# The last blocks of a decoder layer's final stage in two column halves, its final norm scaled on ScalarE and applied in groups of blocks

## The chip, the cores and the metric

One Trainium2 chip, all 8 cores. Each core computes 1024 of the 8192 positions by itself, in two parts of 512 positions. The metric is the device time in microseconds (us) of the slowest core.

A run of all cores is fast or slow: in a slow run the cores of one die (cores 0 to 3 or 4 to 7), or of both, show a lower granted TensorE clock than the others, and the time is longer. Even a fast run can hold a dip of the clock on two cores that costs about 26 us (before's profiled run: 6695.6 and 6695.2 us on cores 4 and 5, 6662.8 to 6679.3 on the six others), and all the effects below are no larger than that. I therefore also read one stretch of each trace, the **last stage**: from the start of the 128x512 fp32 matmul that sums the squares of the first part (it ends that part) to the end of the span. In the trace of the kernel before, this stretch is 287.4 to 287.7 us on all eight cores, while the spans of the same eight cores differ by 33 us. It is a difference of two times in one trace, core by core.

## The reference, cut to what matters

```python
# last sub-layer of the layer (D = 4096, 32 blocks of 128 channels)
ple_gate = sigmoid(rms_norm(x, norm_ple_gate) @ w_ple_gate)      # 4096 x 4096
x = x + rms_norm(ple_gate * (p @ w_ple), norm_ple_post)
```

The post norm needs the sum of squares over all 4096 channels of a position. So no channel of the output can be finished before the last block of the gate matmul is done.

## The kernel before

Channels are on the 128 partitions (32 blocks), positions on the columns. Every weight block is streamed through a ring of 12 slabs of 256 KB whose loads GpSimd issues; x and the output go through SyncE. The program gives each engine its own list of instructions, and in the traces an engine works it off in order: in x5 below the same VectorE instructions in another order take 3.28 us a block in place of 4.95. In the views TensorE is PE, VectorE is DVE, ScalarE is ACT and GpSimd is POOL; PSUM (ps) is the memory that the matmuls write. rstd is the factor that a norm multiplies with, the reciprocal root of the mean square.

```python
def e_job(hf, f, side):              # block f of part hf: 32 + 2 matmuls of 128x512
    bg, be = one_bank(512), one_bank(512)
    def evac_g():                    # gate = sigmoid(psum * rstd)
        O("dve", "tensor_tensor", ... in0=pv(bg), in1=r4.v, op=ALU.mult)
        O("act", "activation", ... func=AF.Sigmoid)
        ...                          # very last block: a tiny Ln, to load its table early
    def evac_e():
        r = R3[hf][f] = alloc(f"R3{hf}_{f}", [512], F32)
        O("dve", "tensor_tensor", ... out=r.v, in0=pv(be), in1=sg.v, op=ALU.mult)
        ...                          # squares: ScalarE Square, then acc += on VectorE
        if f == NCH - 1:
            ...
            if hf == 0:              # first part: its norm runs as "side" steps between
                B.side.extend(last(0, ...))          # the second part's matmuls
                B.side.extend(load_x2(k) for k in range(NKEEP))
    ...

# norm_steps, as used by last(): two VectorE instructions of 128x512 per block
def scaled(k): O("dve", "tensor_tensor", ... in0=m, in1=r.v, op=ALU.mult)
def added(k):  O("dve", "scalar_tensor_tensor", ... in0=m, scalar=gains[:, gp, k:k + 1],
                 in1=x.v, op0=ALU.mult, op1=ALU.add)

for f in range(NCH): e_job(0, f, 14)
for f in range(NCH): e_job(1, f, 14)
B.code(tail)                         # second part: its whole norm after the last matmul
```

The softmax here doesn't subtract the row's maximum and nothing guards it: scores larger than these inputs give would overflow.

## Time and profile before

| | before |
|---|---|
| time, fast runs | 6670.8 to 6671.2 us |
| TensorE busy | 98% of the span |
| chain of waits | 95% TensorE |
| last weight matmul, from the start of the last stage | 237.3 us |
| from there to the end (the tail) | 50.1 us |

The page's first part (busy time, share, instructions) and fourth part (the chain that ended last), kernel before:

```profile
PE 6561.1 (98%) x41283; PEld 4030.5 (60%) x41283; DVE 1975.1 (29%) x2585; ACT 828.2 (12%) x1248; POOL 1352.8 (20%) x2531
...
PE 95%; DMA 1%; DVE 1%; ACT 1%; issue 1%; POOL 0%; DVEq 0%; ACTq 0%; SPq 0%; POOLq 0%
```

The chain says that nearly all of the time is matmuls behind matmuls. What is not is at the two ends. The end, in the timeline of core 4 (start, duration, engine, operation, output and inputs, shape, count; in brackets the engine's idle time before it and what ended it):

```profile
6407.95 1.10 PE L144 MATMUL ps<-sb_arena,sb_ones_f 128*128 128x512 f32 x2 [2.23 <-DVE sb_arena L144]
...
6638.80 1.10 PE L144 MATMUL ps<-sb_arena,sb_ones_f 128*128 128x512 f32 x2 [1.83 <-DVE sb_arena L144]
6639.73 5.56 PE L144 MATMUL ps<-sb_arena,sb_wr 128*128 128x512 bf16 x25
...
6644.97 0.69 DVE L144 TENSOR_TENSOR sb_arena<-ps,sb_arena 128x512 f32<-128x512 f32 x1 [6.42 <-PE ps L144]
6645.75 0.63 ACT L144 ACTIVATE sb_arena<-sb_arena 128x512 f32<-128x512 f32 x1 [8.07 <-DVE sb_arena L144]
6646.40 1.28 ACT L144 ACT_TABLE_LOAD   x1
...
6648.56 0.59 PE L144 MATMUL ps<-sb_arena,sb_ones_b 128*128 128x512 bf16 x1 [3.27 <-ACT sb_arena L144]
...
6650.76 1.29 DVE L144 TENSOR_TENSOR sb_arena<-sb_arena 128x512 f32<-128x512 f32 x2 [3.58 <-ACT sb_arena L144]
6651.97 0.74 DVE L144 SCALAR_TENSOR_TENSOR sb_arena<-sb_arena,sb_cf 128x512 f32<-128x512 f32 x1
...
6689.90 1.40 DVE L144 SCALAR_TENSOR_TENSOR sb_arena<-sb_arena,sb_cf 128x512 f32<-128x512 f32 x2
```

The first line starts the last stage; the second is the fp32 sum of squares of the second part, which waited 1.83 us. The last weight matmuls end near 6645 us. Then comes a chain through VectorE, ScalarE (with a table load of 1.28 us) and one small matmul to 6650.8, and from there 64 VectorE instructions, two a block: 6650.76 to 6691.3 and 40.5 us long. `norm_steps` puts the product of the next block ahead of the sum of this one, so that no instruction needs the result of the one just before it. The last store lands at 6695.6.

The windows view of the same core (start:end, length, busy time and count of PE, PEld, DVE, ACT, POOL, then the granted clock, the DMA share and GB/s):

```profile
6525.00:6550.00 25.00, 25.00 (x117) 11.35 (x116) 7.37 (x12) 5.04 (x8) 9.39 (x18) 1.00 1.01 305
6600.00:6625.00 25.00, 25.00 (x118) 11.30 (x116) 7.20 (x11) 4.41 (x7) 8.76 (x18) 1.00 0.57 166
6650.00:6675.00 25.00, 0.00 (x0) 0.00 (x0) 24.24 (x39) 0.63 (x1) 0.00 (x0) 0.50 0.46 178
```

TensorE is full until the tail, VectorE is full in the tail (24.24 of 25 us) and mostly idle before it. The DMA engines are full (share 1.01) while x and the first part's output move, and at 0.57 when only weights do.

This profiled run itself is no measure of the total: core 4 took 6695.6 us, 24 us more than the timed runs, because its granted clock was 0.81 for 100 us and 0.89 for another 100 (windows view, 500 to 700 us).

### The profile page before, as it was taken

What the parts mean: (1) busy time and instruction counts of PE and PEld (TensorE: products, weight loads), DVE (VectorE), ACT (ScalarE), POOL (GpSimd) and SP (SyncE); (2) the same over time, 40 slices, a digit from 0 to 9 for tenths busy, and PEclk for the clock granted to TensorE, in tenths of its full rate; (3) what the DMA queues carried; (4) which work ended last, traced back from release to release, by engine and by line L of the source; (5) the groups of instructions that cost most, each with busy time, mean ns of one, the idle gap of its engine ahead of it and who ended that gap; (6) DMA issues with size and microseconds to landing.
All of it is one profiled execution on the core that took longest, in us unless ns stands there. A gap on an engine that the chain in (4) does not pass through costs nothing.

```text
span 6695.6 us, 104771 instructions; the slowest of 8 cores (6662.8 to 6695.6 us)
## 1 busy us (share of the span) xinstructions
PE 6561.1 (98%) x41283; PEld 4030.5 (60%) x41283; DVE 1975.1 (29%) x2585; ACT 828.2 (12%) x1248; POOL 1352.8 (20%) x2531
## 2 busy tenths in 40 slices
PE   6999999999999999999999999999999999999996
PEld 4656666666665585866644566665446666544443
DVE  3432311111111125433300133332013333334454
ACT  2550000000001233000000000000000000013311
POOL 1111111111112322311111111111111111233332
PEclk9998999999999999999999999999999999999998
DMA  7557988899887587688899988556875555589885
GB/s 180 82 77 95 116 114 114 117 122 120 116 115 170 158 225 218 176 112 109 110 146 161 156 114 111 77 77 119 163 142 77 77 76 76 138 229 262 236 243 189
DMA packets 377185, 923.25 MB, mean 138 GB/s; under 512 B 49920, under 2 KB 72576, under 8 KB 370944
## 3 DMA queue, kind: packets, MB, share of 16 engines
q0 software_dynamic: 290016, 717.91, 66.2%
q1 hardware_dynamic: 86400, 197.94, 9.5%
q8 instruction: 337, 5.52, 0.3%
q14 instruction: 144, 1.18, 0.1%
q10 hardware_dynamic: 288, 0.70, 0.0%
HBM read 1310.05 MB, written 206.61 MB: 227 GB/s over the span
## 4 chain that ended last, share of the span: by engine, by line
PE 95%; DMA 1%; DVE 1%; ACT 1%; issue 1%; POOL 0%; DVEq 0%; ACTq 0%; SPq 0%; POOLq 0%
PE ps L144 95%; DVE sb_arena L144 1%; ACT sb_arena L144 1%; DMA sb_arena<-w_in 1%; DMA sb_arena<-xs 1%; POOL sb_arena L144 0%; DVEq L143 0%; ACTq L143 0%; ACT L144 0%; DVEq L132 0%; ACT sb_warm L144 0%; SPq L143 0%; POOLq L169 0%
## 5 line engine op out<-in xcount | busy, mean ns | idle before, releaser
L144 PE MATMUL ps<-sb_arena,sb_wr 128*128 128x512 bf16 (+5 forms) x39744 | 6410.8, 323 | 7.5 <-DVE sb_arena L144 4.4
L144 PEld LDWEIGHTS ps<-sb_arena,sb_wr 128*128 128x128 bf16 x39744 | 3890.5, 98 | 2434.0 <-issue 12.8
L144 DVE TENSOR_TENSOR sb_arena<-ps,sb_arena 128x512 f32<-128x512 f32 (+10 forms) x904 | 684.1, 757 | 3995.1 <-PE ps L144 3796.4
L144 ACT ACTIVATE sb_arena<-sb_arena 128x512 f32<-128x512 f32 (+11 forms) x686 | 494.1, 723 | 4627.9 <-DVE sb_arena L144 4511.8
L144 POOL DMA_DIRECT2D sb_wr<-w_up x608 | 322.2, 530 | 1750.5 <-PE ps L144 1679.6
L144 DVE TENSOR_TENSOR sb_arena<-sb_arena 128x512 f32<-128x512 f32 (+8 forms) x545 | 449.6, 837 | 532.6 <-ACT sb_arena L144 503.9
L144 DVE SCALAR_TENSOR_TENSOR sb_arena<-sb_arena,sb_cf 128x1024 f32<-128x1024 f32 (+4 forms) x576 | 593.2, 1031 | 40.8 <-DVE sb_arena L144 0.9
L144 POOL DMA_DIRECT2D sb_wr<-w_in x384 | 205.0, 541 | 1295.7 <-PE ps L144 1295.7
L144 POOL DMA_DIRECT2D sb_wr<-w_down x256 | 135.7, 530 | 666.6 <-PE ps L144 641.7
L144 ACT ACTIVATE sb_arena<-ps 128x512 bf16<-128x512 f32 (+7 forms) x291 | 160.2, 550 | 777.4 <-PE ps L144 770.3
L144 PE MATMUL ps<-sb_arena 128*128 128x296 bf16 (+4 forms) x1216 | 182.0, 267 | 30.4 <-DVE sb_arena L144 17.4
L144 POOL DMA_DIRECT2D sb_wr<-b_out x256 | 137.5, 537 | 339.9 <-PE ps L144 316.4
L144 DVE TENSOR_SCALAR sb_arena<-sb_arena,sb_cf 128x1024 f32<-128x1024 f32 (+3 forms) x320 | 183.5, 602 | 55.5 <-PE ps L144 20.2
L144 POOL DMA_DIRECT2D sb_wr<-b_down x256 | 137.6, 537 | 283.5 <-PE ps L144 251.2
L144 POOL DMA_DIRECT2D sb_wr<-b_pg x256 | 137.6, 537 | 232.2 <-PE ps L144 215.9
L144 PEld LDWEIGHTS ps<-sb_arena 128*128 128x128 bf16 (+1 forms) x1216 | 107.9, 98 | 106.2 <-issue 74.8
L144 POOL DMA_DIRECT2D sb_wr<-b_up x160 | 86.2, 538 | 203.4 <-PE ps L144 190.9
L144 PE MATMUL ps<-sb_arena,sb_ones_b 128*128 128x296 bf16 (+3 forms) x289 | 75.1, 338 | 42.5 <-ACT sb_arena L144 21.4
L144 ACT ACTIVATE sb_arena<-ps,sb_cf 64x386 f32<-64x386 f32 (+3 forms) x112 | 69.8, 624 | 287.1 <-PE ps L144 283.0
L144 ACT ACTIVATE sb_arena<-sb_arena,sb_cf 128x512 bf16<-128x512 f32 (+1 forms) x128 | 90.7, 708 | 0.0
L144 DVE TENSOR_TENSOR sb_arena<-sb_arena,sb_cb 128x512 bf16<-128x512 bf16 (+1 forms) x192 | 64.3, 335 | 65.4 <-ACT sb_arena L144 59.7
L144 POOL DMA_DIRECT2D sb_wr<-w_bp x64 | 33.8, 528 | 194.2 <-PE ps L144 190.6
(31 smaller groups left out, 251.5 us busy)
## 6 DMA issues: line engine op xcount, KB each, us to landing
sb_wr<-w_up POOLq DMA_DIRECT2D x608, 256.0 KB, 4.3
sb_wr<-w_in POOLq DMA_DIRECT2D x384, 256.0 KB, 6.2
sb_wr<-b_out POOLq DMA_DIRECT2D x256, 256.0 KB, 3.0
sb_wr<-b_pg POOLq DMA_DIRECT2D x256, 256.0 KB, 6.5
sb_wr<-w_down POOLq DMA_DIRECT2D x192, 256.0 KB, 6.3
sb_wr<-b_down POOLq DMA_DIRECT2D x192, 256.0 KB, 3.7
sb_wr<-b_up POOLq DMA_DIRECT2D x160, 256.0 KB, 3.8
b_out<-w_out POOLq DMA_DIRECT2D x32, 1024.0 KB, 14.1
```

The lines of the kernel that those rows point to most:

```text
L144: inst = getattr(engine, fn[0])(**fn[1])
```

## The change

The intent is to shorten the tail. The last 8 blocks of the second part are computed in two column halves, first all eight blocks for 256 columns, then all eight for the other 256; their gate weights are read twice. The norm of the first half can then run beside the matmuls of the second half, and only 256 columns are left for the tail. The gain is multiplied in earlier, on ScalarE, so the last two instructions per element are a plain product and a plain sum, done for four blocks at a time (128x1024), the sum right behind its own product (`fin`); in the tail, groups 0 and 4 of eight are given to GpSimd.

```diff
+        NLAST = 8
+        HW = 256
...
+        def half_job(h, f, last, side):            # block f, columns of half h
+            bg = one_bank(HW)
+            be = one_bank(512) if h == 0 else None # w_ple for both halves, once
...
+                gate(pv(bg), bg[0][0], 1, cols, sg)          # VectorE product, ScalarE sigmoid
...
+                    O("dve", "tensor_tensor", [t.b, sg.b], [t.b], ..., op=ALU.mult)
+                if last:
+                    ...                                      # Square in bf16
+                    B.side.extend(last_B(h, last_rstd(h), (t, ap, f)))
+                else:
+                    O("act", "activation", ..., func=AF.Square)
+                    scale_gain(t, ap, f)                     # ScalarE: r *= gain
+                    O("dve", "tensor_tensor", ..., op=ALU.add)   # acc += squares
...
+        def fin(eng, R, x, r, put):                          # a group's final norm
+            O(eng, "tensor_tensor", [R.b, r.b], [R.b], ..., op=ALU.mult)
+            O(eng, "tensor_tensor", [R.b, x.b], [R.b], ..., op=ALU.add)
+            put()
...
+            if h == 0:
+                for g in range(8):
+                    out.append(step(g, "dve"))
+                    if g >= XE:
+                        out.append(load_xb(1, g))
+                return out
+            order = ((0, "pool"), (1, "dve"), (2, "dve"), (3, "dve"), (4, "pool"), (5, "dve"), ...)
...
-        for f in range(NCH):
-            e_job(1, f, 14)
-        B.code(tail)
+        for f in range(NCH - NLAST):
+            e_job(1, f, 24)
+        for f in range(NCH - NLAST, NCH):
+            if f == NCH - 1:
+                B.code(B.drain_side)
+                B.code(lambda: B.side.append(sum_most(0)))   # fp32 sum of the squares so far
+            half_job(0, f, f == NCH - 1, 24)
+        for f in range(NCH - NLAST, NCH):
+            if f == NCH - 1:
+                B.code(lambda: B.side.appendleft(sum_most(1)))
+            half_job(1, f, f == NCH - 1, 18)                 # a side step every 18 matmuls
+        B.code(B.drain_side)
```

The first part's norm is rewritten in the same way (groups of two blocks of 512, all on VectorE).

More of the change, by code (lines that the diff above doesn't have):

```diff
@@ L390, in build_nc @@
         O("dve", "memset", [], [constB], partial=True, ap=ones_b[:], constant=1.0)
+        onesB = constB
         O("dve", "memset", [], [constB], partial=True, ap=ones_f[:], constant=1.0)
@@ L856, in added @@
                     O("act", "activation", [m.b], [q.b], out=q.v, in_=m.v[:, 0:n], func=AF.Square)
-                    h = hout[k] = alloc(f"h_{k}", [n], BF16)
+                    h = hout[k] = alloc(f"h_{k}", [n], BF16, hi=gn == 4)
                     O("act", "activation", [m.b, constB], [h.b], out=h.v, in_=m.v[:, 0:n], func=AF.Copy,
@@ L1150, in build_nc @@
             down_part(1, f, 22)
-        R3 = [{}, {}]
+        NLAST = 8
+        HW = 256
         outB = []
+        RA = {}
+        RB = [{}, {}]
+        XB = [{}, {}]
         def start_E():
@@ L1160, in start_E, with sum_most, run, last_rstd @@
             G["sg"] = [alloc(f"sg{i}", [512], F32, hi=True) for i in range(3)]
+            G["sql"] = [alloc(f"sql{h}", [HW], BF16, hi=True) for h in range(2)]
         warm, warmB = sb("warm", [128, 1], F32)[:], Buf("warm")
-        def sum_most():
-            O("pe", "matmul", [G["acc"].b, constB], [psB[7]], out=ps[:, 7, 0:512], lhsT=ones_f[:], rhs=G["acc"].v,
-              start=True, stop=False)
-        def last_rstd(r):
-            O("pe", "matmul", [G["sqf"].b, constB], [psB[7]], partial=True, out=ps[:, 7, 0:512], lhsT=ones_b[:],
-              rhs=G["sqf"].v.bitcast(BF16)[:, 0:512], start=False, stop=True)
-            rstd_to(r, [(7, 0, 512, 0)])
+        def sum_most(h):
+            def run():
+                O("pe", "matmul", [G["acc"].b, constB], [psB[6 + h]], out=ps[:, 6 + h, 0:HW], lhsT=ones_f[:],
+                  rhs=G["acc"].v[:, h * HW:(h + 1) * HW], start=True, stop=False)
+            return run
+        def last_rstd(h):
+            def run(r):
+                O("pe", "matmul", [G["sql"][h].b, onesB], [psB[6 + h]], partial=True, out=ps[:, 6 + h, 0:HW],
+                  lhsT=ones_b[:], rhs=G["sql"][h].v, start=False, stop=True)
+                rstd_to(r, [(6 + h, 0, HW, 0)])
+            return run
+        def r_of(hf, f):
+            if hf == 0:
+                if f % 2 == 0:
+                    RA[f // 2] = alloc(f"RA{f}", [2, 512], F32)
+                t = RA[f // 2]
+                return [(t, t.v[:, f % 2, :], slice(0, 512))]
+            out = []
+            for h in range(2):
+                if f // 4 not in RB[h]:
+                    RB[h][f // 4] = alloc(f"RB{h}_{f}", [4, HW], F32)
+                t = RB[h][f // 4]
+                out.append((t, t.v[:, f % 4, :], slice(h * HW, (h + 1) * HW)))
+            return out
+        def gate(ap, bank, hf, cols, sg):
+            r4 = G["r4"][hf]
+            n = cols.stop - cols.start
+            O("dve", "tensor_tensor", [psB[bank], r4.b], [sg.b], out=sg.v[:, 0:n], in0=ap, in1=r4.v[:, cols], op=ALU.mult)
+            O("act", "activation", [sg.b], [sg.b], out=sg.v[:, 0:n], in_=sg.v[:, 0:n], func=AF.Sigmoid)
+        def scale_gain(t, ap, f):
+            O("act", "activation", [t.b, constB], [t.b], partial=True, out=ap, in_=ap, func=AF.Copy,
+              scale=gains[:, 5, f:f + 1])
         def e_job(hf, f, side):
@@ L1176, in evac_g @@
             def evac_g():
-                sg, r4 = G["sg"][f % 3], G["r4"][hf]
-                O("dve", "tensor_tensor", bufs(bg) + [r4.b], [sg.b], out=sg.v, in0=pv(bg), in1=r4.v, op=ALU.mult)
-                O("act", "activation", [sg.b], [sg.b], out=sg.v, in_=sg.v, func=AF.Sigmoid)
-                if (hf, f) == (1, NCH - 1):
-                    O("act", "activation", [constB], [warmB], out=warm, in_=epst[:, 0:1], func=AF.Ln)
+                gate(pv(bg), bg[0][0], hf, slice(0, 512), G["sg"][f % 3])
             def evac_e():
@@ L1187, in evac_e @@
                     G["sqf"] = alloc("sqf", [512], F32, hi=True)
-                r = R3[hf][f] = alloc(f"R3{hf}_{f}", [512], F32)
                 sg = G["sg"][f % 3]
-                O("dve", "tensor_tensor", bufs(be) + [sg.b], [r.b], out=r.v, in0=pv(be), in1=sg.v, op=ALU.mult)
-                if (hf, f) == (1, NCH - 1):
-                    O("act", "activation", [r.b], [G["sqf"].b], out=G["sqf"].v.bitcast(BF16)[:, 0:512], in_=r.v,
-                      func=AF.Square)
-                else:
-                    squares(r, 512, G["acc"], G["sqf"], f == 0)
-                if f == NCH - 1:
-                    B.drain_side()
-                    free([h2[hf][c] for c in range(NCH)])
-                    if hf == 0:
-                        free(G["sqf"])
-                    if hf == 0:
-                        B.side.extend(last(0, acc_rstd(G["acc"], ((0, 512),))))
-                        B.side.extend(load_x2(k) for k in range(NKEEP))
-            if (hf, f) == (1, NCH - 1):
-                B.code(lambda: B.side.appendleft(sum_most))
+                ps_ = r_of(hf, f)
+                for t, ap, cols in ps_:
+                    O("dve", "tensor_tensor", bufs(be) + [sg.b], [t.b], partial=True, out=ap,
+                      in0=ps[:, be[0][0], cols], in1=sg.v[:, cols], op=ALU.mult)
+                acc, sqf = G["acc"], G["sqf"]
+                d = acc if f == 0 else sqf
+                for t, ap, cols in ps_:
+                    O("act", "activation", [t.b], [d.b], partial=cols.start > 0, out=d.v[:, cols], in_=ap, func=AF.Square)
+                    scale_gain(t, ap, f)
+                if f > 0:
+                    O("dve", "tensor_tensor", [sqf.b, acc.b], [acc.b], out=acc.v, in0=acc.v, in1=sqf.v, op=ALU.add)
+                if hf == 0 and f == NCH - 1:
+                    B.drain_side()
+                    free([h2[0][c] for c in range(NCH)], sqf)
+                    B.side.extend(last_A(acc_rstd(acc, ((0, 512),))))
+                    B.side.extend(load_xb(h, g) for h, g in xb_early)
             B.one(B.chunk(bg, NCH, lambda k, h: h2[hf][k].v, lambda k: [h2[hf][k].b], evac_g),
@@ L1211, in e_job @@
                           evac_e), B.slabs("w_ple", f, 2))
-        def last(hf, acc):
-            t0 = hf * 512
-            def res(k, t):
-                if hf == 0:
-                    O("sp", "dma_start", [x2B[0][k]], [t.b], dma=f"xin{k % NR}", out=t.v, in_=x2_d[k][:, 0:512])
-            def put(k, m):
-                b = Buf(f"out{hf}_{k}")
-                outB.append(b)
-                O("sp", "dma_start", [m.b], [b], dma=f"out{k % 8}", out=out_d[k][:, t0:t0 + 512], in_=m.v)
-            return norm_steps(512, ((0, 512),), R3[hf], acc, 5, res, put, None, None, lambda: None,
-                              xs=None if hf == 0 else X2)
@@ L1228, in build_nc, with evac, evac_e @@
-        X2 = {}
-        NKEEP = 22
-        def load_x2(k):
+        def half_job(h, f, last, side):
+            bg = one_bank(HW)
+            be = one_bank(512) if h == 0 else None
+            cols = slice(h * HW, (h + 1) * HW)
+            def evac():
+                sg = G["sg"][f % 3]
+                gate(pv(bg), bg[0][0], 1, cols, sg)
+                if last:
+                    O("act", "activation", [onesB], [warmB], out=warm, in_=epst[:, 0:1], func=AF.Ln)
+                t, ap, _ = r_of(1, f)[h]
+                if h == 0:
+                    O("dve", "tensor_tensor", bufs(be) + [sg.b], [t.b], partial=True, out=ap,
+                      in0=ps[:, be[0][0], 0:HW], in1=sg.v[:, 0:HW], op=ALU.mult)
+                else:
+                    O("dve", "tensor_tensor", [t.b, sg.b], [t.b], partial=True, out=ap, in0=ap, in1=sg.v[:, 0:HW],
+                      op=ALU.mult)
+                if last:
+                    q = G["sql"][h]
+                    O("act", "activation", [t.b], [q.b], out=q.v, in_=ap, func=AF.Square)
+                    B.due = 0
+                    B.side.extend(last_B(h, last_rstd(h), (t, ap, f)))
+                else:
+                    O("act", "activation", [t.b], [G["sqf"].b], out=G["sqf"].v[:, 0:HW], in_=ap, func=AF.Square)
+                    scale_gain(t, ap, f)
+                    a = G["acc"]
+                    O("dve", "tensor_tensor", [G["sqf"].b, a.b], [a.b], partial=True, out=a.v[:, cols], in0=a.v[:, cols],
+                      in1=G["sqf"].v[:, 0:HW], op=ALU.add)
+            def evac_e():
+                t, ap, c1 = r_of(1, f)[1]
+                O("act", "activation", bufs(be), [t.b], partial=True, out=ap, in_=ps[:, be[0][0], c1], func=AF.Copy)
+            if h == 0:
+                B.one(B.chunk(be, 2, lambda k, h_: G["pT"][k].v[:, 512:1024], lambda k: [G["pT"][k].b], evac_e),
+                      B.slabs("w_ple", f, 2))
+            B.one(B.chunk(bg, NCH, lambda k, h_: h2[1][k].v[:, cols], lambda k: [h2[1][k].b], evac),
+                  B.slabs("b_pg", f, NCH, cast=G["c_pg"][f]), side=side)
@@ new lines, in fin, with rep_rstd, row @@
+        def fin(eng, R, x, r, put):
+            O(eng, "tensor_tensor", [R.b, r.b], [R.b], out=R.v, in0=R.v, in1=r.v, op=ALU.mult)
+            O(eng, "tensor_tensor", [R.b, x.b], [R.b], out=R.v, in0=R.v, in1=x.v, op=ALU.add)
+            put()
+            free(R, x)
+        def rep_rstd(r, w, n):
+            for i in range(1, n):
+                O("dve", "tensor_copy", [r.b], [r.b], partial=True, out=r.v[:, i, :], in_=r.v[:, 0, :])
+        def row(t, n):
+            v = Tl()
+            v.b, v.v = t.b, t.v[:, 0, :]
+            return v
@@ new lines, in last_A, with ld, start, step @@
+        def last_A(rstd):
+            S = {}
+            def ld(g):
+                if g < NCH // 2:
+                    S[g] = alloc(f"xA{g}", [2, 512], F32, hi=True)
+                    O("sp", "dma_start", [x2B[0][2 * g], x2B[0][2 * g + 1]], [S[g].b], dma=f"xin{g % NR}",
+                      out=S[g].v, in_=x2_d[2 * g:2 * g + 2, :, 0:512].rearrange("k p t -> p k t"))
+            def start():
+                S["r"] = alloc("rpA", [2, 512], F32, hi=True)
+                for g in range(3):
+                    ld(g)
+                rstd(row(S["r"], 512))
+                rep_rstd(S["r"], 512, 2)
+            def step(g):
+                def run():
+                    def put():
+                        b = Buf(f"outA{g}")
+                        outB.append(b)
+                        O("sp", "dma_start", [RA[g].b], [b], dma=f"out{g % 8}",
+                          out=out_d[2 * g:2 * g + 2, :, 0:512].rearrange("k p t -> p k t"), in_=RA[g].v)
+                    fin("dve", RA[g], S[g], S["r"], put)
+                    ld(g + 3)
+                    if g == NCH // 2 - 1:
+                        free(S["r"])
+                return run
+            return [start] + [step(g) for g in range(NCH // 2)]
@@ L1232, in run, with load_xb @@
+        def load_xb(h, g):
             def run():
-                t = X2[k] = alloc(f"x2r{k}", [512], F32)
-                O("sp", "dma_start", [x2B[1][k]], [t.b], dma=f"xk{k % 8}", out=t.v, in_=x2_d[k][:, 512:1024])
-            return run
+                t = XB[h][g] = alloc(f"xB{h}{g}", [4, HW], F32, hi=True)
+                c0 = 512 + h * HW
+                O("sp", "dma_start", [x2B[1][k] for k in range(4 * g, 4 * g + 4)], [t.b], dma=f"xk{(h * 8 + g) % 8}",
+                  out=t.v, in_=x2_d[4 * g:4 * g + 4, :, c0:c0 + HW].rearrange("k p t -> p k t"))
+            return run
@@ new lines, in build_nc, with last_B, start, step @@
+        XE = 2
+        xb_early = [(0, g) for g in range(8)] + [(1, g) for g in range(XE)]
+        def last_B(h, rstd, lastf):
+            S = {}
+            def start():
+                S["r"] = alloc(f"rpB{h}", [4, HW], F32, hi=True)
+                rstd(row(S["r"], HW))
+                scale_gain(*lastf)
+                rep_rstd(S["r"], HW, 4)
+            def step(g, eng):
+                def run():
+                    R = RB[h][g]
+                    def put():
+                        b = Buf(f"outB{h}{g}")
+                        outB.append(b)
+                        c0 = 512 + h * HW
+                        O("sp", "dma_start", [R.b], [b], dma=f"out{g % 8}",
+                          out=out_d[4 * g:4 * g + 4, :, c0:c0 + HW].rearrange("k p t -> p k t"), in_=R.v)
+                    fin(eng, R, XB[h][g], S["r"], put)
+                return run
+            out = [start]
+            if h == 0:
+                for g in range(8):
+                    out.append(step(g, "dve"))
+                    if g >= XE:
+                        out.append(load_xb(1, g))
+                return out
+            order = ((0, "pool"), (1, "dve"), (2, "dve"), (3, "dve"), (4, "pool"), (5, "dve"), (6, "dve"), (7, "dve"))
+            return out + [step(g, e) for g, e in order]
@@ L1239, in build_nc @@
             e_job(0, f, 14)
-        for f in range(NCH):
-            e_job(1, f, 14)
-        def tail():
-            for k in range(NKEEP, NCH):
-                load_x2(k)()
-            B.side.extend(last(1, last_rstd))
-            B.drain_side()
-        B.code(tail)
+        for f in range(NCH - NLAST):
[10 more added lines that the diff above has]
+        B.code(B.drain_side)
         B.run_jobs()
```

## The prediction

> What bounds the kernel now. TensorE: the page gives PE 98% of the span, and the chain of waits is 95% PE. Only two pieces are not PE: the start, and the tail. On core 4 (timeline) the last weight matmul ends at about 6645 us and the span at 6695.6, a tail of about 51 us: 6 us from there to the first scaling (gate, sigmoid, product, table load, square, sum, Ln, Exp), then 64 VectorE instructions of 128x512 in pairs of 1.265 us (40.5 us), then about 4.3 us for the last store.
>
> What the change does. It aims at those 40 us. Only a 256-column half of the second part is left for the tail; the other half's norm runs beside the last matmuls. The gain is multiplied earlier on ScalarE (0.63 to 0.71 us each, which has room: 12% busy), so the two last instructions become plain products and sums over four blocks (128x1024).
>
> Costs on TensorE. 512 columns take 215.5 ns per matmul (465 in 100 us, windows); the 264/258-column stage shows 900 in 100 us, 111 ns. So the split costs 7 ns x 256, about 2 us, plus one more end-of-half wait (before: 1.8 us for the sum of squares): about 3 us in all. Weight loads (98 ns) still hide.
>
> Costs on DMA, which I expect to bind. The 8 blocks' gate weights (8.4 MB) are read twice. In the last 60 us the core must move about 17.3 MB of weights, 3.1 MB of x and 3.7 MB of output, less some 2.6 MB already in the ring: 21.5 MB, or 356 GB/s at full PE speed. The windows where the DMA share is about 1.0 (6425 to 6575 us) move 300 to 310 GB/s, weights and SP traffic about half each. So I estimate 70 us for 60: the PE runs dry mainly in the second half of the split, in total 5 to 13 us. Last weight matmul: about 11 us later than now.
>
> New tail. Lead-in about 5.5 us (256-column forms, same table load, three copies of rstd). Then 6 groups on VectorE. TENSOR_TENSOR 128x1024 takes 1.23 us, and a dependent one starts 0.17 us after its producer (conv stage); a pair costs about 2.6 us, so 15.5 us. GpSimd does 2 groups, 4 instructions[...]. Last store (512 KB) about 5 us. Tail: 26 us[...], from 51.
>
> Sum: tail -16 to -25, earlier stages +5 to +16: about -12 us. Predicted 6659 us, range 6643 to 6676, from 6671. Within 2%: 0.985; faster by over 2%: 0.01; slower: 0.005.
>
> What would show the steps: last 60 us before the tail with PE windows under full, matmuls waiting on DMA of the weight ring, DMA share about 1.0; matmul pace 111 ns where not starved; tail about 30 us[...].
>
> What would make it wrong: DMA delivering over 340 GB/s (then up to -24 us)[...]; new SBUF placement adding waits earlier.

The forecast's sum was -12 us: the tail 16 to 25 us shorter than its 51, the stages before it 5 to 16 us longer. A price for the GpSimd instructions and what they would do to VectorE's beside them made the tail's worse end (16 us shorter). The better end, 26 us or 25 shorter, adds only the lead-in, VectorE's six groups and the last store.

## The result

| | before | after |
|---|---|---|
| fast runs of the first comparison | 6670.8, 6671.0, 6671.2 us | 6670.9, 6672.4, 6674.2 us |
| last stage, eight cores | 287.4 to 287.7 | 288.4 to 288.9 |
| last weight matmul, from the start of the stage | 237.3 | 255.8 to 256.3 |
| tail | 50.1 to 50.3 | 32.6 to 32.7 |

The ratio after to before is 1.0002, 95% interval 0.998 to 1.0025. (Ratios here are the mean time of one kernel's fast runs over that of the other's fast runs of the same rounds, so not quite the ratio of medians.) Executions in which one die ran at a lower clock are left out of the means.

So the tail did get 17.5 us shorter, and 18.5 to 19 us were lost before it. The same two parts of the page after the change show nothing of this:

```profile
PE 6515.7 (98%) x41050; PEld 4050.0 (61%) x41542; DVE 1979.8 (30%) x2571; ACT 894.0 (13%) x1397; POOL 1380.8 (21%) x2567
...
PE 95%; DVE 1%; issue 1%; ACT 1%; DMA 1%; POOL 0%; DVEq 0%; ACTq 0%; SPq 0%; POOLq 0%
```

TensorE's share and the chain are the same to a per cent. The windows of core 4 show where it went:

```profile
6525.00:6550.00 25.00, 24.89 (x116) 11.34 (x116) 7.12 (x13) 7.58 (x16) 8.65 (x17) 1.00 0.65 188
6575.00:6600.00 25.00, 21.77 (x190) 18.52 (x190) 6.75 (x17) 11.16 (x25) 13.96 (x27) 1.00 0.87 270
6600.00:6625.00 25.00, 19.62 (x179) 17.13 (x176) 17.84 (x25) 6.56 (x15) 7.74 (x15) 0.95 0.96 314
6620.00:6634.00 14.00, 0.38 (x2) 0.13 (x2) 9.78 (x14) 3.51 (x8) 0.00 (x0) 0.59 0.89 291
6634.00:6640.00 6.00, 5.40 (x24) 3.71 (x24) 0.43 (x1) 0.51 (x1) 0.00 (x0) 0.54 0.44 124
```

From 6620 to 6634 TensorE did almost nothing (two matmuls), while VectorE was busy 9.8 of 14 us and the DMA share was 0.89. After that the granted clock was 0.54. The timeline of core 4 in that stretch:

```profile
6383.83 1.10 PE L144 MATMUL ps<-sb_arena,sb_ones_f 128*128 128x512 f32 x2 [1.15 <-DVE sb_arena L144]
...
6595.72 23.52 PE L144 MATMUL ps<-sb_arena,sb_wr 128*128 128x256 bf16 x214
...
6612.12 0.42 DVE L144 TENSOR_TENSOR sb_arena<-ps,sb_arena 128x256 f32<-128x256 f32 x1
6612.63 0.42 ACT L144 ACTIVATE sb_arena<-sb_arena 128x256 f32<-128x256 f32 x1 [2.89 <-DVE sb_arena L144]
...
6613.15 0.42 DVE L144 TENSOR_TENSOR sb_arena<-sb_arena 128x256 f32<-128x256 f32 x1 [0.61 <-ACT sb_arena L144]
6613.67 0.42 ACT L144 ACTIVATE sb_arena<-sb_arena 128x256 f32<-128x256 f32 x1 [0.62 <-DVE sb_arena L144]
...
6614.19 1.56 DVE L144 TENSOR_TENSOR sb_arena<-sb_arena 128x256 f32<-128x256 f32 x2 [0.61 <-ACT sb_arena L144]
6615.92 1.23 DVE L144 TENSOR_TENSOR sb_arena<-sb_arena 128x1024 f32<-128x1024 f32 x1 [0.17 <-DVE sb_arena L144]
6617.06 0.42 DVE L144 TENSOR_TENSOR sb_arena<-ps,sb_arena 128x256 f32<-128x256 f32 x1
...
6634.60 1.19 PE L144 MATMUL ps<-sb_arena,sb_ones_f 128*128 128x256 f32 x2 [13.81 <-DVE sb_arena L144]
...
6635.58 4.50 PE L144 MATMUL ps<-sb_arena,sb_wr 128*128 128x256 bf16 x22
```

The matmul that waited is the fp32 sum of the second half, ten matmuls into the last block. It waited 13.81 us on this core, after a wait of 1.16 us for weights (14.9 to 15.1 us and none on the seven others), for VectorE. VectorE was not short of capacity (x5 below does the same work in 3.28 us a block), it was in line: between the gate product of one block (6612.12) and that of the next (6617.06) lie 4.95 us. In it are the block's gate product, a wait for the sigmoid, the block's product, a wait for the square, the addition to the sum, together with the group's final product, and the group's final addition. That is 3.7 us of instructions and 1.2 us of waiting for ScalarE, against 32 matmuls in 3.55 us (111 ns each). VectorE took its list in order here: final-norm instructions that were ready long before stood behind the 0.61 us waits in every block.

More is lost after the long wait: the next 22 weight matmuls took 4.50 us, at the granted clock of 0.54 in the window (4.0 to 4.5 us on the other cores), while in the kernel x5 below, where the wait is 2.5 us, they took 2.56 on five cores. But on x5's cores 4 and 5 the 22 matmuls took 4.23 us after waits of only 2.3 and 2.5 us, so the length of the wait alone does not decide it here.

The tail of core 4 after the change:

```profile
6646.01 1.23 DVE L144 TENSOR_TENSOR sb_arena<-sb_arena 128x1024 f32<-128x1024 f32 x1
6646.42 3.01 POOL L144 TENSOR_TENSOR sb_arena<-sb_arena 128x1024 f32<-128x1024 f32 x1 [33.96 <-DVE sb_arena L144]
6647.41 6.38 DVE L144 TENSOR_TENSOR sb_arena<-sb_arena 128x1024 f32<-128x1024 f32 x2 [0.17 <-DVE sb_arena L144]
6649.64 6.36 POOL L144 TENSOR_TENSOR sb_arena<-sb_arena 128x1024 f32<-128x1024 f32 x2 [0.20 <-POOL sb_arena L144]
...
6653.97 6.38 DVE L144 TENSOR_TENSOR sb_arena<-sb_arena 128x1024 f32<-128x1024 f32 x2 [0.17 <-DVE sb_arena L144]
6656.20 3.07 POOL L144 TENSOR_TENSOR sb_arena<-sb_arena 128x1024 f32<-128x1024 f32 x1 [0.20 <-POOL sb_arena L144]
6660.52 2.36 DVE L144 TENSOR_TENSOR sb_arena<-sb_arena 128x1024 f32<-128x1024 f32 x2 [0.17 <-DVE sb_arena L144]
```

Beside each other both engines' instructions are long: a GpSimd instruction of 128x1024 takes 3.0 to 3.3 us, and the VectorE pairs beside it 6.38 us, where later, alone, a pair takes 2.36.

### The profile page after: what moved, and what is told of

Same layout as the page of the kernel before. It is cut to its first block, busy times and chain, and to the rows that moved or that the text cites. A ratio compares the mean times of both kernels' runs of the same rounds, so it can differ in the third digit from the quotient of the medians.

```text
span 6672.7 us, 105004 instructions; the slowest of 8 cores (6664.6 to 6672.7 us)
## 1 busy us (share of the span) xinstructions
PE 6515.7 (98%) x41050; PEld 4050.0 (61%) x41542; DVE 1979.8 (30%) x2571; ACT 894.0 (13%) x1397; POOL 1380.8 (21%) x2567
## 4 chain that ended last, share of the span: by engine, by line
PE 95%; DVE 1%; issue 1%; ACT 1%; DMA 1%; POOL 0%; DVEq 0%; ACTq 0%; SPq 0%; POOLq 0%
PE ps L144 95%; DVE sb_arena L144 1%; ACT sb_arena L144 1%; DMA sb_arena<-w_in 1%; POOL sb_arena L144 0%; DMA sb_arena<-xs 0%; DVEq L143 0%; ACT L144 0%; ACTq L143 0%; ACT sb_warm L144 0%; SPq L143 0%; POOLq L169 0%
## 5 line engine op out<-in xcount | busy, mean ns | idle before, releaser
L144 DVE TENSOR_TENSOR sb_arena<-ps,sb_arena 128x512 f32<-128x512 f32 (+11 forms) x936 | 685.1, 734 | 3935.3 <-PE ps L144 3670.9
L144 DVE TENSOR_TENSOR sb_arena<-sb_arena 128x512 f32<-128x512 f32 (+10 forms) x556 | 491.1, 897 | 552.2 <-ACT sb_arena L144 508.5
L144 DVE SCALAR_TENSOR_TENSOR sb_arena<-sb_arena,sb_cf 128x1024 f32<-128x1024 f32 (+4 forms) x512 | 546.4, 1068 | 44.4 <-DMA sb_arena<-xr 3.6
L144 ACT ACTIVATE sb_arena<-ps 128x512 bf16<-128x512 f32 (+8 forms) x299 | 162.9, 545 | 774.2 <-PE ps L144 744.1
L144 PE MATMUL ps<-sb_arena 128*128 128x296 bf16 (+4 forms) x1216 | 185.4, 271 | 28.5 <-DVE sb_arena L144 17.2
L144 POOL DMA_DIRECT2D sb_wr<-b_pg x288 | 154.6, 537 | 230.5 <-PE ps L144 204.5
L144 ACT ACTIVATE sb_arena<-sb_arena,sb_cf 128x512 bf16<-128x512 f32 (+3 forms) x224 | 146.3, 653 | 11.0 <-ACT sb_arena L144 2.1
```

Of the source, the lines that this page charges most:

```text
L144: inst = getattr(engine, fn[0])(**fn[1])
```

## The experiments

Two questions were open: what holds up TensorE before the tail (VectorE's order, or DMA as I had predicted), and whether GpSimd helps the tail. All kernels are built on the changed one. The last column is the fp32-sum wait of the second half.

| kernel | last stage, cores | last weight matmul (best core) | tail | wait at the sum |
|---|---|---|---|---|
| before | 287.4 to 287.7 | 237.3 | 50.1 | 1.8 |
| after | 288.4 to 288.9 | 255.8 | 32.6 | 13.8 to 15.1 |
| x1 no GpSimd in the tail | 285.5 to 292.2 | 255.8 | 29.6 | 14.2 to 15.2 |
| x2 no first-half norm (wrong) | 273.5 to 284.6 | 240.8 | 32.6 | 1.5 to 1.8 |
| x3 12 blocks split | 288.5 to 296.1 | 255.4 | 33.0 | 10.4 to 11.8 |
| x4 4 blocks split | 288.4 to 294.6 | 248.9 | 39.5 | 8.8 |
| x5 first-half norm in the gaps | 274.6 to 278.5 | 242.0 | 32.6 | 2.3 to 2.5 |
| x6 x5 and no GpSimd | 273.6 to 275.1, two cores 307, 308 | 244.0 | 29.6 | 2.3 to 2.5 |
| x7 the sum after all matmuls | 285.5 to 286.2 | 238.0 | 45.9 to 47.6 | 11 to 13, after the last weights |
| x8 x6, tail reordered, x earlier | 270.0 to 272.9 | 242.2 | 27.8 | 1.9 to 2.5 |
| x9 x8, sums later, no copies | 262.4 to 264.9; again 262.8 to 266.0 | 236.0 | 26.5 to 29.2 | at most 0.3 |
| x10 no split at all | 283.4 to 290.1 | 237.3 | 45.9 to 47.5 | 2.9 |

Where a row has a wide range, its best cores are the undisturbed ones. The upper ends of x1, x2, x3, x4 and x10 come from single cores that lost 1 to 5 us at one more place, 95 to 99 us into the stage: there VectorE waits for a load of x for the first part's norm, and TensorE then for VectorE (x2, core 2: 6.4 us, and 5.3 us behind it). The profiled run of after showed no such wait of TensorE above 0.5 us, but every core of after had VectorE waiting for x for 9.6 to 11.7 us in that stretch, and none of before had. A smaller loss, of about 1.7 us, is a slower stretch right after one of the short waits (x1, cores 0 and 1: 46 matmuls in 6.85 us, 5.18 on core 4; x10, cores 4 and 7: 30 in 8.32 us, 6.64 on core 1). The ratios of total times of x2, x3, x4 and x7 (1.0004, 1.0004, 1.0041 and 0.9991) all have intervals that contain 1 and decide nothing; the ratios that say more are given below.

### x1: the tail on VectorE alone

```diff
-            order = ((0, "pool"), (1, "dve"), ..., (4, "pool"), ...)
+            order = tuple((g, "dve") for g in range(8))
```

> All eight groups of the tail on VectorE, none on GpSimd. I measure the last stage, from the 128x512 fp32 sum matmul that ends the first part to the end: before 287.4 us, after 288.4 to 288.9 us. Blocking theory[...]: in the trace of after 4 GpSimd and 5 VectorE instructions took 14.3 us together where 9 VectorE instructions alone would take about 11.5; so the tail gets about 3 us shorter, last stage about 285.8, VectorE 128x1024 all near 1.23 us. Rival (the VectorE instructions were stretched for another reason, and GpSimd did a quarter of the work for free): four more VectorE instructions, tail about 5 us longer, last stage about 294.

Measured: correct; the tail is 29.6 to 29.7 us on every core, 3.0 less than after's 32.6, and the undisturbed cores need 285.5 to 285.9 us. Groups of VectorE instructions in the tail of core 4, first of after, then of x1 (shape, count, busy us, mean ns, idle time before):

```profile
L144 DVE TENSOR_TENSOR sb_arena<-sb_arena 128x1024 f32<-128x1024 f32 x12 | 22.3, 1892 | 1.1 <-DVE sb_arena L144 1.0
```

```profile
L144 DVE TENSOR_TENSOR sb_arena<-sb_arena 128x1024 f32<-128x1024 f32 x17 | 20.2, 1223 | 1.7 <-DVE sb_arena L144 1.6
```

The mean of after's twelve instructions is 1892 ns: the four beside GpSimd take 3.1 to 3.4 us each, the eight others 1.23. In x1 (16 in the tail, and the last one of the first half's norm) the mean is 1223 ns. So taking a quarter of the work away from VectorE made it slower, by the 3 us that the blocking theory said: 16 instructions on VectorE alone take 20.3 us, 12 there and 4 on GpSimd 23.35. Why the instructions slow each other was not shown. The ratio of total times, 1.0013 (0.9975 to 1.0051), cannot show 3 us.

### x2: no final norm of the first half on VectorE (wrong result)

```diff
+                    if h == 0:
+                        put(); free(R, XB[h][g])     # store unscaled
+                    else:
                         fin(eng, R, XB[h][g], S["r"], put)
```

> Wrong result on purpose: the 16 VectorE instructions of the first half's final norm are left out, its stores and loads stay. VectorE theory (PE waits 14 to 15 us for the sum of squares because VectorE, in order, takes 4.95 us per block with a final norm in it, against 3.5 us of matmuls): that wait falls to about 2 us. DMA theory: with stores no longer held up by VectorE, weights, x and stores would need over 400 GB/s, so the PE waits for weights instead, by 8 to 12 us, and the last stage hardly shortens. If the VectorE theory is all of it, last stage about 274 us; if DMA is the next limit right behind it, 280 to 286.

Measured: the wait at the sum fell to 1.5 to 1.8 us on all cores, and the best core needed 273.5 us. That is the VectorE theory's number, and no wait for weights of 5 us showed (the longest was 1.45). The run says less about DMA than I had meant it to: without the VectorE step nothing held SyncE back, so it issued most of those stores and loads earlier, beside the first halves (on core 4 all but two of the eight stores before 6570 us; in after all eight from 6604.8 to 6644.4).

### x3 and x4: 12 and 4 split blocks

```diff
-        NLAST = 8
+        NLAST = 12        # x3;  4 in x4
```

> Last 12 blocks split in place of 8; all else as after. VectorE theory: the second halves give 42 us of matmuls for the same eight final norms, four blocks have none, so the backlog is worked off before the sum: its wait falls from 14 to about 2 us, +1 us for the narrower matmuls; last stage about 277 us, 11 us less than before. DMA theory: 4 MB more weights to read; PE waits grow, last stage 292 or more.

> Last 4 blocks split in place of 8. VectorE theory: 14 us of matmuls against the same eight final norms; only about four of them fit before the end, the side steps that are not popped run on VectorE after the last block; so the loss moves, but stays: tail plus wait about 12 us more than after, last stage 298 to 302 us. DMA theory: half the weights are re-read, the wait shrinks, last stage below 284.

Measured: both theories missed both numbers. With 4, 8 and 12 split blocks the undisturbed cores need 288.4 to 288.9 us, always the same. Read in the traces, this is what a line that is bound by VectorE looks like. In x3, once the eight final norms are done, a block takes VectorE 2.55 us against 3.55 of matmuls, so the backlog shrinks by only 1 us a block, and three to four such blocks are left: 14.9 becomes 11. I had taken it to vanish. In x4 only three of the eight final norms come before the sum; one runs beside the last matmuls and four after the last block, back to back at 2.53 us each and partly in the time in which VectorE waits for rstd. The wait is 6 us shorter (8.8) and the tail 7 us longer (39.5). I had overlooked that outside the blocks a final norm costs no waits for ScalarE. The DMA theory fails in both directions: half the re-read weights did not help and half as many again did not hurt.

### x5 and x6: the same instructions in another order

In x5, each group's product goes between a block's gate product and its product, and the group's sum ahead of the addition of squares, the two places where VectorE waits for ScalarE. x6 adds x1's edit.

```diff
                 gate(pv(bg), bg[0][0], 1, cols, sg)
+                if FILL and not last:
+                    FILL.popleft()()         # product of one group of the first half
...
                     a = G["acc"]
+                    if FILL:
+                        FILL.popleft()()     # its sum with x, and its store
                     O("dve", "tensor_tensor", ..., op=ALU.add)
```

> Same instructions as after, other order: the two VectorE instructions of each of the first half's final norms are put into the two places of each later block where VectorE waits for ScalarE (between gate and product, and before the sum of squares). VectorE theory: per block 3 x 0.36 + 2 x 1.16 = about 3.5 us in place of 4.95, as long as the matmuls (3.55 us); the PE's wait for the sum falls from 14 to 15 us to about 3; last stage about 277 us. If instead DMA is the next limit once the stores come at that pace (the first rival), PE waits for weights of 5 us or more show up and the last stage stays above 282.

> x5 and no GpSimd in the tail: both theories of before together. The two gains are in different stages and should add: 277 - 3 = about 274 us for the last stage, 13 less than before the change, so about 6657 us in a fast run.

Measured: both correct. x5's wait at the sum is 2.3 to 2.5 us and its last stage 274.6 to 278.5 us. Its fast runs are 6660.3 and 6660.4 us; the ratio is 0.9976 (0.994 to 1.0012). One block in the timeline of core 0, and the sum matmul:

```profile
6600.24 0.42 DVE L144 TENSOR_TENSOR sb_arena<-ps,sb_arena 128x256 f32<-128x256 f32 x1
6600.58 3.02 DVE L144 TENSOR_TENSOR sb_arena<-sb_arena 128x1024 f32<-128x1024 f32 x4
...
6603.52 0.42 DVE L144 TENSOR_TENSOR sb_arena<-ps,sb_arena 128x256 f32<-128x256 f32 x1
...
6617.89 0.67 PE L144 MATMUL ps<-sb_arena,sb_ones_f 128*128 128x256 f32 x2 [2.52 <-DVE sb_arena L144]
```

From one gate product to the next are 3.28 us in place of 4.95, with no instruction taken away: the line of four instructions ("x4", 3.02 us) runs without a gap, although two of the four need ScalarE's result. That decides the first question. No wait of TensorE for weights shows on any core. On core 4 the sum waited no longer than on core 0 (2.31 us), but the 22 matmuls after it took 4.23 us in place of 2.56, at a granted clock of 0.74 over the 8 us from 6616:

```profile
6615.54 0.75 PE L144 MATMUL ps<-sb_arena,sb_ones_f 128*128 128x256 f32 x2 [2.31 <-DVE sb_arena L144]
6616.13 4.23 PE L144 MATMUL ps<-sb_arena,sb_wr 128*128 128x256 bf16 x22
```

In x6 six cores took 273.6 to 275.1 us (tail 29.6). The tail's gain of 3.0 us is there in full, but the best core is only 1.0 ahead of x5's: on all six the 22 matmuls after the sum took 3.5 to 4.4 us, against 2.56 on x5's core 0. That the total meets the 274 expected is therefore partly luck, since x5 came out 2.4 under its own 277. The other two, cores 2 and 3, took 308 and 307 us. The windows of core 2 in x6:

```profile
6400.00:6450.00 50.00, 49.70 (x223) 22.40 (x226) 31.70 (x42) 14.43 (x31) 18.29 (x34) 0.97 1.02 307
6500.00:6550.00 50.00, 49.74 (x189) 20.75 (x191) 12.32 (x24) 13.81 (x30) 15.56 (x29) 0.81 0.62 174
```

Between those two windows the granted clock fell to 0.81, and the second holds 189 matmuls; cores 0 and 1 of the same die had clock 1.00 and 234 matmuls there (they had begun the last stage 13 to 20 us later than cores 4 to 7). The run counts as fast. It is why the ratio of x6 (0.9996) says nothing, and why I read the last stage.

### x7: the sum after all weight matmuls

```diff
-            if f == NCH - 1:
-                B.code(lambda: B.side.appendleft(sum_most(1)))
             half_job(1, f, f == NCH - 1, 18)
+        B.code(lambda: sum_most(1)())
```

> As after, but the fp32 sum matmul of the second half comes after all weight matmuls and not ten matmuls into the last block. VectorE theory: the wait only shows at the sum, its cause is VectorE's backlog, so the PE finishes its weights about 17 us earlier, but VectorE comes to the last block's gate only when its backlog is done; the last stage shortens by no more than the 5.6 us from the end of that wait to the last weight matmul: about 283 us. If the sum's place were the cause, it would shorten by some 14 us, to 275.

Measured: 285.5 to 286.2 us, 3 us less than after. The weights are done at 238.0 to 239.7 us, 16 to 18 us earlier, and then TensorE waits 11 to 13 us for VectorE. So the sum is only where the backlog is noticed. The gain is smaller than 5.6 because without that side step the last group's final norm (2.6 us) got in front of the last block's gate product in VectorE's list.

### x8 and x9: a version better than both

x8 is x6 with the next group's product ahead of this group's sum in the tail, so that no instruction needs the result of the one before it (the order that the kernel before has), and with five loads of x ahead in the first part's norm in place of three.

```diff
-                    ld(g + 3)                # after fin(...) of group g
+                    ld(g + 5)
...
+            def tail():
+                mul1(0)
+                for g in range(8):
+                    if g < 7:
+                        mul1(g + 1)
+                    add1(g)
```

> x6, and in the tail the next group's product ahead of this group's sum (saves 0.17 us a group, 1.3 us), and five loads of x ahead in place of three in the first part's norm (takes away the waits of PE some 95 us into the last stage that single cores showed in the runs so far; no change in the best core). Last stage about 272.5 us on every core, a fast run about 6655 us, 0.2% below both kernels.

x9 places the sums later in the last blocks and reads one copy of rstd for all four blocks of a group instead of making three copies of it.

```diff
-                B.code(lambda: B.side.append(sum_most(0)))
-            half_job(0, f, f == NCH - 1, 24)
+                B.code(lambda: (B.side.append(sum_most(0)), setattr(B, "due", 0)))
+            half_job(0, f, f == NCH - 1, 29.5 if f == NCH - 1 else 24)
...                                            # the same for the second half
-                rep_rstd(S["r"], HW, 4)
...
-  in1=S["r"].v
+  in1=S["r"].v.to_broadcast([128, 4, HW])
```

> x8 with the three short PE waits around the halves' ends made shorter (fp32 sums 30 matmuls into the last block and not 4 to 10, the small sum 24 and not 18 matmuls into the next) and rstd read once per group in place of three copies. In x8 the waits are 2.1, 1.0 and 2.5 us and the copies 1.1 us of the tail. If VectorE keeps up, last stage about 265 us in the best core (x8: 270.0), a fast run about 6650 us. If the waits only move to the last block's gate, because VectorE is behind there, it stays at 268 or more.

> The same kernel as x9_best2, whose only fast run had two cores that lost 26 us before the last stage, as two cores of the profiled run of before had. Last stage 262 to 265 us again; a fast run without such a loss at 6645 to 6650 us, against 6670 to 6672 of before on the same chip.

Measured: both correct. x8 took 6655.4 and 6656.7 us in its fast runs (before: 6670.2 to 6688.2; ratio 0.997, 0.9933 to 1.0006), 270.0 to 272.9 us in the last stage, and no core lost time 95 us into it. Of the 3.6 us by which its best core is ahead of x6's, the tail's new order is 1.8; the rest is mostly the clock after the sum, 22 matmuls in 2.57 us (core 0) against 4.10 (core 0 of x6). x9's first set had a single fast run, with the clock at 0.81 on cores 0 and 1 for 100 us (6674.3 us, no ratio), but its last stage was 262.4 to 264.9 us. Sent again, its four fast runs took 6649.6, 6649.9, 6650.3 and 6651.9 us against 6671.2 to 6679.1 of before: ratio 0.9966, interval 0.9948 to 0.9984. That is the best kernel, about 20 us or 0.3% ahead of before (and of after's fast runs, which were not taken beside it). The tail on core 6 of its second set:

```profile
6620.71 18.25 DVE L144 TENSOR_TENSOR sb_arena<-sb_arena 128x1024 f32<-128x1024 f32 x16 [0.39 <-ACT sb_arena L144]
```

Sixteen instructions in one row, 18.25 us, 1.14 us each. In x1, where every sum follows its own product, sixteen took 20.3 us.

DMA comes into view only here. A window of core 0 of x8, in the second halves:

```profile
6600.00:6610.00 10.00, 10.00 (x85) 8.53 (x83) 9.86 (x16) 4.01 (x9) 4.84 (x9) 0.88 1.00 348
```

The share is 1.00 at 348 GB/s and the granted clock is 0.88. On cores 4 to 6 of x8 the last weight matmul comes 3 us later than on core 0, and the windows of the two dies tell why. First core 0, then core 4:

```profile
6600.00:6608.00 8.00, 8.00 (x68) 6.84 (x66) 7.86 (x14) 3.17 (x7) 4.35 (x9) 0.88 0.99 352
6608.00:6616.00 8.00, 7.82 (x70) 6.66 (x68) 7.42 (x11) 3.10 (x7) 0.50 (x1) 0.97 1.00 308
6616.00:6624.00 8.00, 3.07 (x24) 2.45 (x24) 3.99 (x7) 2.85 (x6) 0.00 (x0) 1.00 1.07 346
```

```profile
6600.00:6608.00 8.00, 8.00 (x68) 6.86 (x67) 8.00 (x13) 3.61 (x8) 4.33 (x9) 0.89 1.00 322
6608.00:6616.00 8.00, 8.00 (x63) 6.63 (x62) 6.88 (x11) 2.69 (x6) 1.04 (x2) 0.81 0.99 312
6616.00:6624.00 8.00, 5.70 (x37) 4.21 (x36) 3.51 (x6) 1.34 (x3) 0.00 (x0) 0.80 1.07 329
```

The DMA share is the same. The clock takes about 1.2 us from core 0 in these 24 us (0.12 + 0.03 of 8 us) and about 4.0 from core 4 (0.11 + 0.19 + 0.20), and the waits view of cores 4 to 6 lists no wait of TensorE for weights at all. So it is the clock that costs those 3 us, not DMA: the 216 matmuls before the sum took 25.6 to 26.3 us on cores 4 to 7, 24.5 to 24.8 on cores 0 to 3 and 23.7 in x1, and the 22 after it 4.2 to 4.4 us on cores 4 to 6 and 2.57 on the others. In x5 (24.6 to 26.3 us) and x6 (24.9 to 28.5) those 216 are slower than in x1 too; what brings the dips on was not tested, and up to 1.2 us of x9's lead over x8's best core is owed to it. In x9 single cores wait for weights, up to 1.4 us at a time and 0 to 2.6 us in all.

### x10: the rest of the change without the split

`NLAST = 0`, the second part's norm written as the first part's, in 16 groups of two blocks of 512, in the tail, all on VectorE, products one group ahead.

> The rest of the change without the split: gains on ScalarE, groups of two blocks of 512, no block in halves, no GpSimd; the second part's norm in the tail as before the change. Tail: lead-in 6 us, 32 instructions of 1.14 us = 36.5, last store 3.6: 46 us in place of 50.1; last stage about 283.5 (before 287.4, after 288.7). So the split as it stands would cost about 5 us against this, and x8's order of it win 13.

Measured: correct, 283.4 to 286.0 us on seven cores (one lost 3.7 us at the 95 us place), tail 45.9 to 47.5 us. So the gains on ScalarE and the groups are worth about 4 us, if the products stay one group ahead as in the kernel before: 32 instructions in 36.4 us against 64 in 40.5. In the change's own order they are worth nothing, by an estimate from x1: there a pair of 128x1024 takes 2.53 us for 1024 columns, and before, two pairs of 128x512 take the same 2.53. Against x10 the split as it was written cost 5 us, of which GpSimd (3.0, x1) and the order in the tail (1.8, x8 against x1) make up nearly all when added; the split in x9's order gains 20.

## Why the prediction was right or wrong, point by point

- **What bounds the kernel, and the size of the tail**: right. TensorE to the end, then 40 us of VectorE.
- **Costs on TensorE**: about right, 4 us where 3 was said. In the first halves a block took 3.92 us, 32 narrow and two wide matmuls, as estimated from 111 ns; with 3.55 in the second half that is 7.47 us a block against 7.33 before, 1.1 us for eight. The waits at the end of the first half were 2.1 and 1.0 us where 1.8 was said.
- **"Costs on DMA, which I expect to bind"**: this is the step that failed. TensorE did stand still in the second half of the split, but for VectorE and not for weights: the only wait for weights of over 0.5 us in after's last stage is 1.2 us, on one core, where 5 to 13 us were forecast. Two things were wrong in it. The 300 to 310 GB/s that I took for the ceiling were means of 25 us windows in which TensorE never waited for weights; the trace of before itself has 339 GB/s over 10 us (core 4, 6567 to 6577 us), and x8 shows 348. And the stores were not there to compete, because VectorE, late itself, released them late (core 4: one every 4.9 to 5.1 us from 6617 to 6632, the last at 6644.4). What DMA costs when VectorE is in time, x5 and x9 show: at most 2.6 us of waits for weights on a core.
- **What I did not cost at all, and what took the place of that step**: VectorE in the last 28 us of matmuls. "The other half's norm runs beside the last matmuls" stands in the prediction without a price. I counted its work for the tail, but not the 16 final-norm instructions that the split moves under the matmuls. They are 20 us of work, and in an in-order list they also turn each block's two waits for ScalarE into lost time: 4.95 us a block against 3.55. The matmuls could hide the moved work only if VectorE had that much free time in the right order. x2 (work away), x5 (order changed) and x3, x4 (number of blocks changed, no effect) agree on this.
- **"Last weight matmul: about 11 us later"**: it was 18.5 to 19. The wait at the sum is 13.8 to 15.1 us where 1.8 was before, so some 13 more; the slower clock after it (0.54) adds 2, the end of the first half 3.1, the narrower matmuls 1.1.
- **New tail, 16 to 25 us shorter**: right, at 32.6 us, between the two ends. Beside GpSimd's instructions (3.0 to 3.3 us) VectorE's took 3.1 to 3.4 us in place of 1.23; the 26 us of the better end had not counted that.
- **Sum**: tail -17.5 as predicted, earlier stages +18.5 to +19 where +5 to +16 was said, so +1 in place of -12. "Within 2%" held; the time, 6671 to 6674, is within the stated range of 6643 to 6676 only when read from the fast runs, and that is the width of the range, not the argument: the gain forecast did not come.

## What to carry to other kernels

When work is moved from a tail under a busy engine, count it on the engine that has to do it there, per block and with the waits of its in-order list; here a block took 4.95 us under matmuls of 3.55, and the backlog of eight such blocks showed at the next wait, as 13.8 to 15.1 us. Put the moved instructions into the places where that engine waits for another one anyway: here the same instructions in another order gained 10 to 14 us. When instructions are merged into larger ones, keep dependent ones apart: here that alone was worth 2 us in 20. And before giving part of a VectorE row to GpSimd, measure it: here VectorE's instructions took 3.1 to 3.4 us beside GpSimd's in place of 1.23, and the help cost 3 us.

## What the runs show of single instructions and of the clock

- Order mattered at the same number of instructions: sixteen VectorE instructions of 128x1024, each sum behind its own product, took 20.3 us (x1), the same sixteen with independent neighbours 18.25 us (x9). The next instruction starts 0.17 us after the recorded end of a producer (x1), and about 0.08 us before the end of an instruction that it does not need (x9).
- A GpSimd TENSOR_TENSOR of 128x1024 beside VectorE's took 3.0 to 3.3 us, VectorE's beside it 3.1 to 3.4 us in place of 1.23 (after); GpSimd alone was not run.
- The slow runs show whole dies as low as 0.81; in fast runs the means of all eight cores are 0.986 to 0.997, and a dip to 0.81 in x6 took cores 2 and 3 while cores 0 and 1 of their die stayed at 1.00.
